# Gathering a mixture-of-experts input in other PSUM banks, with slot tiles ahead of rounding remainders and weight rows in 4 KB pieces

## The chip, the cores and the metric

The kernel runs on one core of one Trainium2 chip. A core has a matrix engine (TensorE, PE in the profile; PEld is its weight load), a vector engine (VectorE, DVE), a scalar engine (ScalarE, ACT), GpSimd (POOL) and SyncE (SP), which here issues nearly all DMAs. They run side by side, each in its own program order, and wait for each other through semaphores. Matmul results land in PSUM, 8 banks of 2 KB in each of 128 partitions. The metric is the device time of one execution in microseconds (us).

## What is computed

Two layers on 256 tokens of width 1024 in fp32: a gated linear attention, then a differential attention, each followed by a layer norm, a mixture of experts and another layer norm. Only the mixture of experts is touched:

```
def hier_moe(x, w_group, b_group, w_router, b_router, w_gate, w_up, w_down):
    ...
    y = jnp.zeros_like(t)
    for e in range(MOE_EXPERTS):            # 16 experts, 1024 -> 512 -> 1024
        hdn = jax.nn.silu(t @ w_gate[e]) * (t @ w_up[e])
        y = y + combine[:, e:e + 1] * (hdn @ w_down[e])
    return y.reshape(B, S, D)
```

Each token goes to the two best of the four experts in its best group; `combine` is zero elsewhere.

## The kernel before

Both layers call `moe`. It runs all 16 experts on at most 64 tokens each; fuller experts get another round in a loop at the end, which this input does not enter, and layer 1 runs one extra block of 64, so 17. An expert's tokens are picked by a matmul with a one-hot matrix (a **slot tile**, `OH`), four experts at a time: that is `gather_group(g)`, for g = 0 before the first expert and for g = 1, 2, 3 ahead of experts 4, 8 and 12. The gather is exact: `split_x` makes of a 128-wide slice of the normalized input `xa` (both token blocks) a rounded high part (`act.activation` on ScalarE, line 534) and the remainder, the **low part** (`eng.tensor_sub` on VectorE, line 535), in a tile `xs` of which there are four. For each of the 8 slices, four matmuls (high part and low part, each for two token blocks) are summed in PSUM (line 553). Two slices share a bank. ScalarE and VectorE then scale, shift and store them as `xg` (lines 560 and 562); the one on ScalarE follows the one on VectorE, since both read the same bank.

PSUM tiles come from three rings: `pA` (4 banks, held by the sums `y` during `moe`), `pB` (2) and `pC` (2). Gather, transposes (`tr_part`, `s_prep`) and half of the down product use `pC`; the gate and up product (`gu_part`, line 610) and the other half of the down product (line 638) use `pB`. A ring hands out its banks in turn, and a writer waits until the last reader of that bank is through.

An expert needs 6 MB of weights: 8 transfers of 512 KB for gate and up (line 282) and 2 of 1 MB for down (line 286). SP issues them in a fixed order into a ring of 16 slots of 1 MB (3 more for the start of each layer), as slots come free, with at most eight transfers under way. The gate and up rows of slot j are `j * 256` to `j * 256 + 255`, partition p holding rows p and p + 128, each 2 KB long. A scheduler puts the instructions of each engine in order from the program text and the `issue_after` hints (`with after(...)`).

Of the kernel before, what the change touches and what calls it, by code (L numbers as in the profile page):

```python
# [10 lines left out]
F32 = mybir.dt.float32  # L11
# [10 lines left out]
KC = D // 128  # L22
# [14 lines left out]
P_G, P_B, P_GN, P_GS, P_WR = 0, 32, 64, 72, 73  # L37
# [6 lines left out]
def body(ctx, tc, x, w_in, wa_out, kv_w, wq, wb_out, wg, wu, wd, gate2, rows, rtab, lng, lnb, cblob, pblob, onehot, out):  # L44
    nc = tc.nc
    pe, act, dve, pool, sp = nc.tensor, nc.scalar, nc.vector, nc.gpsimd, nc.sync

    const = ctx.enter_context(tc.tile_pool(name="const", bufs=1))
# [15 lines left out]
    def pB():  # L64
        return psum.tile([128, 512], F32, tag="B", bufs=2, name=nm("pB"))

    def pC():
        return psum.tile([128, 512], F32, tag="C", bufs=2, name=nm("pC"))
# [7 lines left out]
    xa = const.tile([128, 2, D], F32, name="xa")  # L76
# [5 lines left out]
    iota = cb[:, C_IO:C_IO + 64]  # L82
    pb = const.tile([128, NPB], F32, name="pb")
    rw = const.tile([1, R_LAM], F32, name="rw")
    lnr = const.tile([64, 256], F32R, name="lnr")
    sel_r = const.tile([64, 32], F32R, name="sel_r")
    ones_r = const.tile([128, 128], F32R, name="ones")
# [178 lines left out]
    def load_moe(layer, res):  # L266

        n, spares = 0, []
        for e in range(E):
            gu, dn = [], []  # L270
            res.append((gu, dn))
            for j in range(6):
                if n == RING:
                    spares = yield
                if e == 8 and j == 0:
                    yield
                n += 1
                t = spares.pop(0) if spares else ring_slot()
                if j < 4:
                    t = t.rearrange("p (g k f) -> p g k f", g=2, k=2)  # L280
                    for gi, w in enumerate((wg, wu)):
                        sp.dma_start(t[:, gi], w[layer, e, j * 256:j * 256 + 256].rearrange("(k p) f -> p k f", p=128))
                    gu.append(t)
                else:
                    t = t.rearrange("p (k f) -> p k f", k=2)
                    sp.dma_start(t, wd[layer, e, (j - 4) * 256:(j - 4) * 256 + 256].rearrange("(k p) f -> p k f", p=128))
                    dn.append(t)
        yield
# [32 lines left out]
    rt = sm([32, 8], "rt", bufs=1)  # L321
    sp.dma_start(rt, rtab)
    sp.dma_start(pb, pblob)
    sp.dma_start(rw, rows[0:1, 0:R_LAM])
    for i, w in enumerate((lng, lnb)):
        for j in range(2):
# [142 lines left out]
    def moe(layer, M, lg, rstd, nr, fold, side=None):  # L469
        with tc.tile_pool(name=f"moe{layer}", bufs=1) as mp:  # L470
# [42 lines left out]
            after = lambda i: tc.issue_after(getattr(i, "ins", i)) if i is not None else contextlib.nullcontext()  # L513

            def one_hot(g):
                n = 5 if layer and g == 3 else 4
                OH[g] = mp.tile([128, 2, n, 64], F32R, tag="OH", bufs=2, name=nm("OH"))
                for b in range(2):
                    mm = dve.tensor_tensor(OH[g][:, b, 0:4],
                                      posm[:, b, 4 * g:4 * g + 4].unsqueeze(2).broadcast_to([128, 4, 64]),  # L520
                                      iota.unsqueeze(1).broadcast_to([128, 4, 64]), op=ALU.is_equal)
                    if n == 5:
                        dve.tensor_scalar(OH[g][:, b, 4], iota, extra[1][:, b:b + 1], None, op0=ALU.is_equal)
                return mm
            gcol, bcol = P_G + 16 * layer, P_B + 16 * layer

            lows = []

            def split_x(k, eng, hold=None):

                t = mp.tile([128, 2, 2, 128], F32R, tag="xs", bufs=4, name=nm("xs"))
                x_ = xa[:, :, k * 128:k * 128 + 128]
                with after(hold):
                    act.activation(t[:, 0], x_, AF.Copy)
                lows.append(eng.tensor_sub(t[:, 1], x_, t[:, 0]))
                return t

            def gather_group(g, hold=None, xs=()):

                n = 5 if layer and g == 3 else 4  # L540
                t = mp.tile([128, KC, 256], F32, tag="xg", bufs=1, name=nm("xg"))
                if n == 5:
                    tx = spare_tile(1, [128, KC, 64], F32, "xg4")
                    xg_tiles[4] = tx
                xs = list(xs)
                for k in range(KC):
                    if n == 5 or k % 2 == 0:
                        p = pC()
                    if k >= len(xs):
                        xs.append(split_x(k, dve, hold))  # L550
                    o = p[:, 0:320] if n == 5 else p[:, k % 2 * 256:k % 2 * 256 + 256]
                    for q in range(4):
                        pe.matmul(o, xs[k][:, q // 2, q % 2], OH[g][:, q % 2].rearrange("p e s -> p (e s)"), start=q == 0, stop=q == 3)  # L553
                    for i in range(k, k + 1) if n == 5 else (k - 1, k) if k % 2 else ():
                        src = p[:, 0:256] if n == 5 else p[:, i % 2 * 256:i % 2 * 256 + 256]
                        gc, bc = (pb[:, c + i:c + i + 1] for c in (gcol, bcol))
                        if n == 5:
                            dve.tensor_scalar(tx[:, i], p[:, 256:320], gc, bc, op0=ALU.mult, op1=ALU.add)
                        if n == 5 or i % 2:
                            act.activation(t[:, i], src, AF.Identity, scale=gc, bias=bc)  # L560
                        else:
                            dve.tensor_scalar(t[:, i], src, gc, bc, op0=ALU.mult, op1=ALU.add)
                xg_tiles[g] = t
# [156 lines left out]
            def reload(ei, tile_, eng, et):  # L720

                ev = nc.values_load(ei[0:1, 0:1], engines=[et], min_val=0, max_val=E - 1,
                                    skip_runtime_bounds_check_because="sixteen less a maximum of sixteen down to one")
                ws = []
                for j in range(6):
                    t = tile_(j)
                    if j < 4:
                        t = t.rearrange("p (g k f) -> p g k f", g=2, k=2)
                        for gi, w in enumerate((wg, wu)):
                            eng.dma_start(t[:, gi], w[layer, bass.ds(ev, 1), j * 256:j * 256 + 256].rearrange("e (k p) f -> p (e k) f", p=128))  # L730
                    else:
                        t = t.rearrange("p (k f) -> p k f", k=2)
                        eng.dma_start(t, wd[layer, bass.ds(ev, 1), (j - 4) * 256:(j - 4) * 256 + 256].rearrange("e (k p) f -> p (e k) f", p=128))
                    ws.append(t)
                return ws[:4], ws[4:]

            def overflow(left, base, rev):

                ei, q, cwx = pick(left, base, rev)
                ws, wdn = reload(ei, lambda j: spare_tile(1 + j % 2, [128, 2048], F32, nm("W")), pool, mybir.EngineType.Pool)  # L740
                oh = mp.tile([128, 2, 64], F32, tag="ohw", bufs=2, name=nm("ohx"))
                for b in range(2):
                    dve.tensor_scalar(oh[:, b], iota, q[:, b:b + 1], None, op0=ALU.is_equal)
                st, wsx, _ = s_prep(lambda b: oh[:, b], 64, cwx)
                p = pC()
                pv = p.rearrange("p (k s) -> p k s", k=KC)
                for k in range(KC):
                    for b in range(2):
                        pe.matmul(pv[:, k], xa[:, b, k * 128:k * 128 + 128], oh[:, b], start=b == 0, stop=b == 1)
                xg = mp.tile([128, KC, 64], F32, tag="o", bufs=2, name=nm("xgx"))  # L750
                gv, bv = (pb[:, c:c + KC].unsqueeze(2).broadcast_to([128, KC, 64]) for c in (gcol, bcol))
                dve.tensor_mul(xg, pv, gv)
                dve.tensor_add(xg, xg, bv)
                p = pB()
                gu_part(ws, range(4), lambda k: xg[:, k], p, 2)
                ht, _ = tr_part(act_part(p, 2), 2)
                scatter(st, down_part(wdn, ht, wsx, 2)[0], True)

            xs0 = [split_x(k, dve) for k in range(4)]
            act.activation(sm([128, 2], "warm"), xs0[3][:, 0, 0, 0:2], AF.Exp, scale=0.0)  # L760
            one_hot(0)
            gather_group(0, None, xs0)
            with after(lows[3]):
                cw = combine()
# [1 line left out]
            for e in range(E + layer):  # L766
# [8 lines left out]
                p = pB()  # L775
# [50 lines left out]
            if layer == 0:  # L826
                p = pB()
# [187 lines left out]
    for j in range(2):  # L1015
# [9 lines left out]
        else:  # L1025
            t = mp.tile([128, 2, 4, S], F32R, tag="xhi", name="ogT1")
# [191 lines left out]
```

## Time and profile before

| | |
|---|---|
| median of 3 runs | 770.43 us (769.76 to 772.49) |
| the profiled execution, its own time | 771.24 us |
| its span, first to last instruction | 769.3 us |
| TensorE busy | 727.1 us (95%) |
| VectorE, ScalarE busy | 357.4 us (46%), 296.8 us (39%) |
| read from HBM | 245.77 MB |

Times inside the execution count from the start of the span; layer 0's mixture of experts lies at about 131 to 366 us, layer 1's at about 502 to 758 us. The 1.9 us between the profiled time and its span lie outside the instructions.

### The profile page before, as it was taken

The numbers are of one execution on the slowest core, as the hardware profiler recorded it, in microseconds if no ns is written. First come the engines' busy times: TensorE is split into PE (matmuls) and PEld (weight loads), VectorE is DVE, ScalarE is ACT, GpSimd is POOL, SyncE is SP. The second block draws the span as 40 slices with busy tenths as digits, with TensorE's granted clock in tenths as the row PEclk, the third lists the DMA queues.
The fourth block names the chain that finished last, engine by engine and source line by source line (L and its number), as shares of the span: only waits on it lengthen the run. The fifth ranks groups of instructions, "written<-read, shape, count | busy, mean of one in ns | idle before, by whom it ended". The sixth has DMA issues, their size and how long they took to land. (4 is left out here: it accounts for less than half of the span.)

```text
span 769.3 us, 10560 instructions
## 1 busy us (share of the span) xinstructions
PE 727.1 (95%) x3743; PEld 407.8 (53%) x3743; DVE 357.4 (46%) x959; ACT 296.8 (39%) x651; POOL 8.9 (1%) x21
## 2 busy tenths in 40 slices
PE   7999998999999999999999999999999999999993
PEld 5898776434333434434798877753343343343331
DVE  3655766333263332322758877654235332332225
ACT  4554766323212322222666656552232232232123
POOL 2200000000000000000000000000000000000000
PEclk9999999999999999999999999999999999999997
DMA  7999957599999999999999355619999999999951
GB/s 226 312 384 388 337 191 262 181 397 394 367 387 392 393 396 395 393 393 367 290 364 359 111 174 209 220 62 389 394 381 395 393 363 384 395 395 393 392 200 55
DMA packets 131934, 247.57 MB, mean 322 GB/s; under 512 B 7932, under 2 KB 38117, under 8 KB 131750
## 3 DMA queue, kind: packets, MB, share of 16 engines
q1 hardware_dynamic: 131270, 244.68, 87.6%
q0 software_dynamic: 176, 1.59, 0.5%
q8 instruction: 31, 0.51, 0.3%
q10 hardware_dynamic: 432, 0.59, 0.2%
q14 instruction: 25, 0.20, 0.1%
HBM read 245.77 MB, written 2.63 MB: 323 GB/s over the span
## 5 line engine op out<-in xcount | busy, mean ns | idle before, releaser
L610 PE MATMUL pB<-W,xg 128*64 128x512 f32 x1056 | 263.6, 600 | 0.0
L610 PEld LDWEIGHTS pB<-W,xg 128*64 128x64 f32 x1056 | 77.3, 138 | 137.9 <-issue 132.3
L638 PE MATMUL pB<-W,ht 128*64 128x512 f32 x248 | 112.6, 594 | 0.0
L638 PE MATMUL pC<-W,ht 128*64 128x512 f32 x248 | 111.5, 592 | 0.0
L647 DVE SCALAR_TENSOR_TENSOR o<-pB,wst,o 64x512 fp32r<-64x512 f32 x31 | 23.1, 744 | 145.3 <-ACT o L646 145.3
L119 DVE TENSOR_TENSOR lo<-W,hi 128x512 fp32r<-128x512 f32 x96 | 66.4, 696 | 37.0 <-PE pA L128 23.9
L118 ACT ACTIVATE hi<-W 128x512 fp32r<-128x512 f32 x96 | 59.3, 629 | 48.3 <-PE pA L129 27.8
L646 ACT ACTIVATE o<-pB,wst 64x512 fp32r<-64x512 f32 x31 | 21.2, 682 | 129.6 <-PE pC L638 101.8
L619 DVE TENSOR_TENSOR hd<-sl,pB 128x256 f32<-128x256 f32 x33 | 13.9, 421 | 102.5 <-ACT sl L617 102.5
L617 ACT ACTIVATE sl<-pB 128x256 f32<-128x256 f32 x33 | 12.7, 385 | 126.0 <-PE pB L610 126.0
L638 PEld LDWEIGHTS pB<-W,ht 128*64 128x64 f32 x248 | 33.3, 137 | 52.4 <-issue 49.3
L553 PE MATMUL pC<-OH,xs 128*128 128x256 f32 (+1 forms) x256 | 39.7, 308 | 7.4 <-DVE ht L629 3.8
L670 PE MATMUL pA<-o,st 128*128 128x512 f32 x132 | 40.9, 431 | 4.3 <-DVE o L664 2.1
L553 PEld LDWEIGHTS pC<-OH,xs 128*128 128x128 f32 x256 | 34.8, 203 | 17.8 <-DVE ht L629 5.2
L638 PEld LDWEIGHTS pC<-W,ht 128*64 128x64 f32 x248 | 33.9, 137 | 19.4 <-issue 18.2
L670 PEld LDWEIGHTS pA<-o,st 128*128 128x128 f32 x132 | 22.4, 191 | 33.3 <-issue 23.5
L129 PE MATMUL pA<-x1Thi,lo 128*128 128x256 f32 x128 | 36.1, 288 | 1.4 <-DVE lo L119 1.2
L127 PE MATMUL pA<-x1Thi,hi 128*128 128x256 f32 x128 | 36.7, 288 | 0.0
L128 PE MATMUL pA<-x1Tlo,hi 128*128 128x256 f32 x128 | 36.2, 284 | 0.0
L128 PE MATMUL pA<-lo,xThi 128*128 128x384 f32 (+1 forms) x96 | 34.3, 357 | 0.0
L129 PE MATMUL pA<-hi,xTlo 128*128 128x384 f32 (+1 forms) x96 | 34.3, 357 | 0.0
L127 PE MATMUL pA<-hi,xThi 128*128 128x384 f32 (+1 forms) x96 | 34.2, 362 | 0.0
(338 smaller groups left out, 1086.2 us busy)
## 6 DMA issues: line engine op xcount, KB each, us to landing
W<-in_moe_w_gate_dram SPq DMA_DIRECT2D x132, 512.0 KB, 11.2
W<-in_moe_w_up_dram SPq DMA_DIRECT2D x132, 512.0 KB, 11.0
W<-in_moe_w_down_dram SPq DMA_DIRECT2D x66, 1024.0 KB, 12.0
W<-in_a_w_in_dram SPq DMA_DIRECT2D x16, 256.0 KB, 5.6
W<-in_a_w_in_dram SPq DMA_DIRECT2D x4, 1024.0 KB, 17.8
W<-in_a_w_out_dram SPq DMA_DIRECT2D x4, 1024.0 KB, 14.4
W<-in_kv_w_dram SPq DMA_DIRECT2D x4, 1024.0 KB, 8.8
W<-in_b_w_q_dram SPq DMA_DIRECT2D x16, 256.0 KB, 5.4
```

Of the source, the lines that this page charges most:

```text
L118: act.activation(hi, src, AF.Copy)
L119: dve.tensor_sub(lo, src, hi)
L127: pe.matmul(o, l[0], r[0], start=first, stop=False, skip_group_check=skip)
L128: pe.matmul(o, l[0], r[1], start=False, stop=False, skip_group_check=skip)
L129: pe.matmul(o, l[1], r[0], start=False, stop=last, skip_group_check=skip)
L553: pe.matmul(o, xs[k][:, q // 2, q % 2], OH[g][:, q % 2].rearrange("p e s -> p (e s)"), start=q == 0, stop=q == 3)
L610: mm = pe.matmul(p[c * m:c * m + m, 0:2 * fw].rearrange("p (g f) -> p g f", g=2), xg(k), w[:, :, kk, c * fw:c * fw + fw], start=k == 0, st ...
L619: anchor[1] = dve.tensor_mul(h, sl, p[:, fw:2 * fw])
L638: mm = pe.matmul(p[2 * c // nt][c * m:c * m + m, 0:w], ht[:, q % n, (q // n) * m:(q // n) * m + m], wd_[q // 2][:, q % 2, c * w:c * w + w] ...
L646: act.activation(hi, src, AF.Copy, scale=ws[a:a + m, 0:1])
L647: dve.scalar_tensor_tensor(lo, src, ws[a:a + m, 0:1], hi, op0=ALU.mult, op1=ALU.subtract)
L670: mm = pe.matmul(y[b][c], st[:, b * 128:b * 128 + 128], o[c], start=False, stop=last, skip_group_check=True)
```

## The change

Four edits. The gather's PSUM tiles come from `pB` and `pC` in turn, two from each. At the start of `moe` the second half of the slot tile and the first low part stand ahead of the other three low parts, which wait for it (`later`, `rest`). The gate and up rows of slot j are now rows 8p + 2j and 8p + 2j + 1 for partition p, adjacent in memory, so that one piece is 4 KB; pieces of neighbouring partitions are 16 KB apart. So that the input's columns match these rows, slice k of the gather now takes columns 8q + k: `xa_r` reads every eighth fp32 number of `xa`, and the scale and shift columns are loaded for that order into `ngb`, by four small transfers on POOL's queue.

```diff
+    ngb = const.tile([128, 2, 2, KC], F32, name="ngb")
...
-                        sp.dma_start(t[:, gi], w[layer, e, j * 256:j * 256 + 256].rearrange("(k p) f -> p k f", p=128))
+                        sp.dma_start(t[:, gi], w[layer, e].rearrange("(p r) f -> p r f", r=KC)[:, 2 * j:2 * j + 2])
...
+    for layer in range(2):
+        for c, w in enumerate((lng, lnb)):
+            pool.dma_start(ngb[:, layer, c], w[layer, 0].rearrange("(p r) -> p r", r=KC))
...
-            gcol, bcol = P_G + 16 * layer, P_B + 16 * layer
+
+            xa_r = xa.rearrange("p b (q r) -> p b r q", r=KC)
+            gbr = ngb[:, layer]
...
-            def split_x(k, eng, hold=None):
+            def split_x(k, eng, hold=None, later=False):
...
-                x_ = xa[:, :, k * 128:k * 128 + 128]
+                x_ = xa_r[:, :, k]
                 with after(hold):
                     act.activation(t[:, 0], x_, AF.Copy)
-                lows.append(eng.tensor_sub(t[:, 1], x_, t[:, 0]))
+                low = lambda: lows.append(eng.tensor_sub(t[:, 1], x_, t[:, 0]))
+                if later:
+                    return t, low
+                low()
                 return t
...
                     if n == 5 or k % 2 == 0:
-                        p = pC()
+
+                        i = k if n == 5 else k // 2
+                        p = pC() if i // 2 % 2 else pB()
...
-                        gc, bc = (pb[:, c + i:c + i + 1] for c in (gcol, bcol))
+                        gc, bc = (gbr[:, c, i:i + 1] for c in range(2))
...
-            xs0 = [split_x(k, dve) for k in range(4)]
+            xs0, rest = [split_x(0, dve)], []
+            for k in range(1, 4):
+                t, low = split_x(k, dve, later=True)
+                xs0.append(t)
+                rest.append(low)
             act.activation(sm([128, 2], "warm"), xs0[3][:, 0, 0, 0:2], AF.Exp, scale=0.0)
-            one_hot(0)
+
+            with after(one_hot(0)):
+                for low in rest:
+                    low()
             gather_group(0, None, xs0)
```

The overflow loop and its reload of weights are changed in the same way and are not shown.

How the instructions now stand, at three places. First VectorE at the start of layer 0's `moe`, before: `OH` is the slot tile (one row for each token block), `xs` the low parts, `xg` the evacuation of gathered slices, the small tiles `mx`, `ex`, `comb`, `s` and `sg` the combine weights.

```order
L510 SCALAR_TENSOR_TENSOR posm_1694<-sel_1685,pC_1688 128x32
L519 TENSOR_TENSOR OH_1710<-posm_1694,cb 128x256
L535 TENSOR_TENSOR xs_1696<-xa,xs_1696 128x256
L535 TENSOR_TENSOR xs_1699<-xa,xs_1699 128x256
L535 TENSOR_TENSOR xs_1702<-xa,xs_1702 128x256
L535 TENSOR_TENSOR xs_1705<-xa,xs_1705 128x256
L519 TENSOR_TENSOR OH_1710<-posm_1694,cb 128x256
```

And VectorE there after the change, up to the third evacuation (in the changed file line 523 writes the slot tile, 541 the low parts, 573 evacuates):

```order
L523 TENSOR_TENSOR OH_1712<-posm_1699,cb 128x256
L541 TENSOR_TENSOR xs_1701<-xa,xs_1701 128x256
L523 TENSOR_TENSOR OH_1712<-posm_1699,cb 128x256
L541 TENSOR_TENSOR xs_1704<-xa,xs_1704 128x256
L541 TENSOR_TENSOR xs_1706<-xa,xs_1706 128x256
L541 TENSOR_TENSOR xs_1708<-xa,xs_1708 128x256
L579 TENSOR_REDUCE mx_1775<-lg_1650 128x10
L573 TENSOR_SCALAR xg_1718<-pB_1719,ngb 128x256
L581 TENSOR_TENSOR ex_1777<-lg_1650,mx_1775 128x40
L573 TENSOR_SCALAR xg_1718<-pB_1730,ngb 128x256
L541 TENSOR_TENSOR xs_1742<-xa,xs_1742 128x256
L541 TENSOR_TENSOR xs_1749<-xa,xs_1749 128x256
```

The slot tile's second half moved ahead of three low parts; two evacuations now stand ahead of the low parts of slices 4 to 7.

Second, TensorE at the same place, before (line 553 gathers, line 610 is the first expert's product):

```order
L553 MATMUL pC_1725<-OH_1710,xs_1705 128x256 x4
L610 MATMUL pB_1785<-W_168,xg_1713 64x512
L553 MATMUL pC_1736<-OH_1710,xs_1737 128x256 x4
L553 MATMUL pC_1736<-OH_1710,xs_1744 128x256 x4
L553 MATMUL pC_1753<-OH_1710,xs_1754 128x256 x4
L553 MATMUL pC_1753<-OH_1710,xs_1761 128x256 x4
```

And after (564 gathers, 621 is the product):

```order
L564 MATMUL pB_1730<-OH_1712,xs_1708 128x256 x4
L564 MATMUL pC_1741<-OH_1712,xs_1742 128x256 x2
L621 MATMUL pB_1790<-W_173,xg_1718 64x512
L564 MATMUL pC_1741<-OH_1712,xs_1742 128x256 x2
L564 MATMUL pC_1741<-OH_1712,xs_1749 128x256 x4
L564 MATMUL pC_1758<-OH_1712,xs_1759 128x256 x4
L564 MATMUL pC_1758<-OH_1712,xs_1766 128x256 x4
```

Slices 0 to 3 moved to `pB`, slices 4 to 7 stay in `pC`; the product's first matmul slid two matmuls later.

Third, TensorE at the gather for experts 4 to 7 of layer 0, before (line 626 is the transpose of the last expert's hidden values, in `pC`):

```order
L594 MATMUL pC_1999<-ident_r,ohw_1996 128x128 x2
L626 MATMUL pC_2006<-ident_r,hd_1990 128x128 x2
L553 MATMUL pC_2015<-OH_2011,xs_2016 128x256 x4
L553 MATMUL pC_2015<-OH_2011,xs_2023 128x256 x4
L553 MATMUL pC_2032<-OH_2011,xs_2033 128x256 x4
L553 MATMUL pC_2032<-OH_2011,xs_2040 128x256 x4
L610 MATMUL pB_2083<-W_992,xg_2014 64x512
```

And after (605 and 637 are the transposes):

```order
L605 MATMUL pC_2004<-ident_r,ohw_2001 128x128 x2
L637 MATMUL pC_2011<-ident_r,hd_1995 128x128 x2
L564 MATMUL pB_2020<-OH_2016,xs_2021 128x256 x4
L564 MATMUL pB_2020<-OH_2016,xs_2028 128x256 x4
L564 MATMUL pB_2037<-OH_2016,xs_2038 128x256 x4
L564 MATMUL pB_2037<-OH_2016,xs_2045 128x256 x4
L564 MATMUL pC_2054<-OH_2016,xs_2055 128x256 x4
L564 MATMUL pC_2054<-OH_2016,xs_2062 128x256 x4
```

The first two banks of the gather are no longer the two that the transposes have just written.

## Rows read from the trace of the kernel before

**Rows 1.** The page: busy time by engine, and DMA by 40 slices.

```profile
PE 727.1 (95%) x3743; PEld 407.8 (53%) x3743; DVE 357.4 (46%) x959; ACT 296.8 (39%) x651; POOL 8.9 (1%) x21
...
DMA  7999957599999999999999355619999999999951
GB/s 226 312 384 388 337 191 262 181 397 394 367 387 392 393 396 395 393 393 367 290 364 359 111 174 209 220 62 389 394 381 395 393 363 384 395 395 393 392 200 55
```

**Rows 2.** All waits, summed: waiter <- releaser: us in total, times, longest.

```profile
PE pC L553 <- DVE ht L629: 3.8, 6, 0.6
...
PEld pB L610 <- DMA W<-in_moe_w_gate_dram: 1.6, 7, 0.3
```

**Rows 3.** TensorE's timeline, first gather of layer 0: start, length, what [idle before].

```profile
132.64 0.51 PE L553 MATMUL pC<-OH,xs 128*128 128x256 f32 x2
134.27 3.36 PE L553 MATMUL pC<-OH,xs 128*128 128x256 f32 x14 [1.12 <-DVE OH L519]
...
138.65 2.18 PE L553 MATMUL pC<-OH,xs 128*128 128x256 f32 x16
140.75 7.08 PE L610 MATMUL pB<-W,xg 128*64 128x512 f32 x30
```

**Rows 4.** Windows there: length, busy PE, PEld, DVE, ACT, POOL, PEclk, DMA, GB/s.

```profile
135.00:136.00 1.00, 1.00 (x7) 1.00 (x6) 0.50 (x4) 0.42 (x1) 0.00 (x0) 0.50 0.00 0
138.00:139.00 1.00, 0.98 (x5) 0.35 (x4) 1.00 (x4) 1.00 (x3) 0.00 (x0) 1.00 0.00 0
```

**Rows 5.** VectorE's and ScalarE's timelines there.

```profile
132.11 0.42 DVE L519 TENSOR_TENSOR OH<-posm,cb 128x256 fp32r<-128x256 f32 x1
132.46 1.42 DVE L535 TENSOR_TENSOR xs<-xa,xs 128x256 fp32r<-128x256 f32 x4
133.80 0.41 DVE L519 TENSOR_TENSOR OH<-posm,cb 128x256 fp32r<-128x256 f32 x1
134.13 0.18 DVE L568 TENSOR_REDUCE mx<-lg 128x10 f32<-128x40 f32 x1
...
136.17 0.54 DVE L562 TENSOR_SCALAR xg<-pC,pb 128x256 f32<-128x256 f32 x1
...
130.96 1.32 ACT L534 ACTIVATE xs<-xa 128x256 fp32r<-128x256 f32 x4
```

**Rows 6.** TensorE's timeline, gathers for experts 4, 12 (layer 0) and 12 (layer 1).

```profile
187.55 2.18 PE L553 MATMUL pC<-OH,xs 128*128 128x256 f32 x16 [0.63 <-DVE ht L629]
...
192.82 1.50 PE L610 MATMUL pB<-W,xg 128*64 128x512 f32 x5
...
308.88 2.18 PE L553 MATMUL pC<-OH,xs 128*128 128x256 f32 x16 [0.58 <-ACT xg L560]
...
684.91 1.64 PE L553 MATMUL pC<-OH,xs 128*128 128x320 f32 x8 [0.45 <-ACT xg L560]
686.79 0.85 PE L553 MATMUL pC<-OH,xs 128*128 128x320 f32 x4 [0.25 <-ACT xg L560]
```

**Rows 7.** Two lines of the program, min/median/max ns of one instruction.

```profile
L376 DVE TENSOR_REDUCE rsum<-wrg x2: 423/435/447, 21.6 to 29.9; 128x20 f32<-128x160 f32 x2
...
L497 DVE TENSOR_REDUCE rank<-cmp x2: 319/320/320, 130.5 to 502.0; 128x40 f32<-128x160 f32 x2
```

**Rows 8.** Windows with DMA alone: length, PEclk, DMA share, GB/s.

```profile
276.00:285.00 9.00, 1.00 1.05 386
334.00:339.00 5.00, 1.00 1.03 405
361.00:388.00 27.00, 1.00 1.15 291
```

**Rows 9.** Layer 0's last weights: issue on SP, us to landing (median), first use.

```profile
341.82 1.74 SPq L286 DMA_DIRECT2D W<-in_moe_w_down_dram  x2
...
W<-in_moe_w_down_dram SPq DMA_DIRECT2D x2, 1024.0 KB, 12.0
...
359.79 0.43 PE L658 MATMUL pB<-W,ht 128*64 128x256 f32 x1 [0.63 <-DVE ht L629]
```

**Rows 10.** The page: a queue of small transfers, packets, MB, share of 16 engines.

```profile
q10 hardware_dynamic: 432, 0.59, 0.2%
```

More of the change, by code (lines that the diff above doesn't have):

```diff
@@ L729, in reload @@
                         for gi, w in enumerate((wg, wu)):
-                            eng.dma_start(t[:, gi], w[layer, bass.ds(ev, 1), j * 256:j * 256 + 256].rearrange("e (k p) f -> p (e k) f", p=128))
+                            eng.dma_start(t[:, gi], w[layer, bass.ds(ev, 1)].rearrange("e (p r) f -> p (e r) f", r=KC)[:, 2 * j:2 * j + 2])
                     else:
@@ L748, in overflow @@
                     for b in range(2):
-                        pe.matmul(pv[:, k], xa[:, b, k * 128:k * 128 + 128], oh[:, b], start=b == 0, stop=b == 1)
+                        pe.matmul(pv[:, k], xa_r[:, b, k], oh[:, b], start=b == 0, stop=b == 1)
                 xg = mp.tile([128, KC, 64], F32, tag="o", bufs=2, name=nm("xgx"))
-                gv, bv = (pb[:, c:c + KC].unsqueeze(2).broadcast_to([128, KC, 64]) for c in (gcol, bcol))
+                gv, bv = (gbr[:, c].unsqueeze(2).broadcast_to([128, KC, 64]) for c in range(2))
                 dve.tensor_mul(xg, pv, gv)
```

## The prediction

> **What bounds the kernel now.** The page first [rows 1]: TensorE (PE) is busy 95% of the span, VectorE (DVE) 46%, ScalarE (ACT) 39%. Moving work off PE is not on offer here; what can go is time in which PE stands still, and time in which it runs at half its clock. The page's DMA slices stand near 390 GB/s through both mixtures of experts, so the weights keep the queues full there, and the table of waits says whether PE feels it [rows 2]: PE waited for gate and up weights 1.6 us in seven times, never over 0.3. Faster weights alone are thus worth at most 1.6 us. The same table has six waits, 3.8 us, of gather matmuls (line 553) in `pC` for the copy `ht` that empties `pC` after the transposes: 0.63 us for each gather of experts 4, 8 and 12 in two layers.
>
> Then the start of layer 0's `moe` on PE's timeline [rows 3]: two gather matmuls at 132.64, then 1.12 us idle for the second half of `OH`, then 14 matmuls in 3.36 us. The next sixteen take 2.18 us, 0.136 each; at that rate fourteen are 1.9. The windows say why [rows 4]: after the idle stretch the granted clock is 0.50 (1.2 GHz) at 135 us, 1.00 (2.4 GHz) at 138. About 1.4 us is lost to the clock, beside the idle. DVE's timeline shows who is late [rows 5]: first half of `OH` at 132.11, four lows at 132.46 to 133.88, second half at 133.80.
>
> **The change, part by part.**
>
> **The start.** PE resumed 0.47 us after the second half of `OH` began (134.27 against 133.80). With one low ahead of it instead of four, that half begins at 132.80 and PE resumes at 133.27. If PE is dense from there, 14 gathers of 0.136 (1.90), the 1.02 us that lie between the two halves of the gather (137.63 to 138.65) and the last sixteen (2.18, less the 0.08 by which records overlap, since the product begins at 140.75) end near 138.3 instead of 140.75: 2.4 us a layer is the most that the reordering gives. DVE may not keep up. Its lows now read every eighth number, and no row has such a low. Below, it costs nothing. Above, the nearest row is a reduce of 160 elements: strided 435 ns (line 376), contiguous 319 ns (line 497) [rows 7]; 116 ns over 160 elements is 0.72 ns each, 0.185 us for a low's 256. I take this, the only strided row: a low goes from 0.335 (1.34 us for four starts) to 0.52. DVE's chain from 132.11 is then `OH` 0.335, low 0.52, `OH` 0.335, three lows 1.56, `mx` 0.20, `xg` 0.46, `ex` 0.20, `xg` 0.46, four lows 2.08, 0.35 until PE sees the last one, two matmuls 0.27, and 0.2 for banks (lengths are the distances between starts in [rows 5], which are a little shorter than the records; `ex` as `mx`): 6.97 us, the gather done at 139.1. Gain 140.75 - 139.1 = 1.65 a layer, 3.3 in two. ACT's highs read strided too; they were four in 1.32 us from 130.96, and with the same 0.185 each end at 133.0, where the third and fourth are wanted only at 134: hidden by the first half of `OH` and the first low. PE's idle stretch shrinks from 1.12 to about 0.45, and I take it that the clock stays at 1.00.
>
> The Trainium skill bears on the strided low ("Vector Engine (DVE) Microarchitecture Reference", section "Measured stream behaviour on trn2"): full rate needs runs of two adjacent 4-byte words, and a small step at every element was measured at 2.50 ns a column against 1.054. By that a low would cost 0.37 us more, not 0.185, and the sum below would come to about 1 us; the rows' 0.72 ns is half of it, for a reduce.
>
> **The groups.** At experts 4, 8 and 12 the first two banks come from `pB`, last read by a product's activation, and not from the two that `ht` is still leaving [rows 6]. At most all goes: six times 0.63, and at expert 12 in layer 0 the 0.58 behind ACT's `xg`, in layer 1 0.45 and 0.25: 5.1 us. At least nothing. For expert 4: PE ran dry at 187.55 - 0.63 = 186.92 and began the product at 192.82, 5.9 us; without the wait 5.27. In that time DVE must do the four lows that its ring of four doesn't let it do ahead (4 x 0.52) and four evacuations (4 x 0.46), 3.9 us, and with 0.35 of lag, four matmuls and the last evacuation comes to 5.1 to 5.4: just about PE's own time. I take 0.55 of 0.63 at the four of experts 4 and 8, 0.48 at expert 12 in layer 0, 0.5 in layer 1 (its five-slot gather takes a bank per slice): 3.2 us.
>
> **What it adds.** Four transfers on POOL's queue, each 128 pieces of 32 bytes. A queue of small pieces is in the rows [rows 10]: 432 packets for 0.2% of sixteen engines, 0.2% x 769.3 x 16 / 432 = 57 ns a packet. 512 are 1.8 us if all sixteen engines stand still for it while the first x rows load; nothing, if they fall into a gap. They are issued beside other small loads, and I take 0.4. The longer lows also stretch DVE where it is dense, about the gathers' tails: three or four lows of 0.185 off cover once a layer, 0.2, so 0.4.
>
> **Pieces of 4 KB.** Windows with DMA alone [rows 8]: 386 GB/s where gate and up dominate (2 KB pieces), 405 where it is `down` (4 KB already), 291 where pieces are 512 bytes. So gate and up may gain 5%. PE doesn't wait for them [rows 2]; layer 0's last weights are issued at 341.82, land 12.0 us after their issue, near 355, and are used at 359.79 [rows 9]. That margin of 4.8 us is what hides this edit, and it grows. I cost it at nothing.
>
> **The sum** is 3.3 + 3.2 - 0.4 - 0.4 = 5.7 us. The profiled execution took 771.24, 1.9 of it outside its span; 771.24 - 5.7 = 765.5. The median of the runs shown, 770.43, is 0.8 below the profiled one, so I forecast 764.7.
>
> **The rivals.** A measurement of this kernel tells about 0.5% from no change, 3.85 us: faster is below 766.6, slower above 774.3.
>
> *The strided reads are free.* Then DVE is ahead everywhere and both upper bounds hold: 2 x 2.4 + 5.1 = 9.9, 760.5. For it: a DVE low at 0.335 is far from any rate that its reads need to set, and two reduces on different lines are a thin row [rows 7]. Against it: that row.
>
> *The strided reads double a low*, 0.335 to 0.67. The start's chain is 1.2 us longer than mine, gain 0.5 a layer; the four slices on DVE's path in a group cost 0.6 more, leaving 0.2 of 0.63; 1.0 + 0.8 - 0.8 = 1.0, so 769.4. What speaks for it is that a low reads two inputs and writes one [rows 5], the reduce only reads. The skill's rule named above is the same case by another figure, and no row here shows it.
>
> *The clock falls all the same.* The idle stretch doesn't vanish, and before the first gather PE has little to do in either kernel. Then 1.4 us is lost in each layer as now: 5.7 - 2.8 = 2.9, 767.5. Against it: the fall followed the 1.12 us, and gathers behind the 0.63 us waits still took 2.18 for sixteen [rows 6].
>
> *Gate and up come slower.* Pieces are longer, but neighbouring partitions' pieces are now 16 KB apart instead of following each other, which no row here has. Thirteen experts of 4.19 MB in layer 0 take 141 us at 387 GB/s. The margin of 4.8 us [rows 9] less the 2.9 that layer 0 gains is 1.9; what goes beyond, PE waits. Layer 1 taken alike, 2 x (X - 1.9) must pass 5.7 + 3.85 to make the kernel slower: X = 6.7 us, at 369 GB/s. At the middle of the rows' 386 and 291 (338), X is 20 and the time 801; at 386 nothing happens. For it: DMA is full throughout [rows 1], so any loss shows. Against it: the windows' order, by piece size alone [rows 8].
>
> The Trainium skill lists a case of this kind ("DMA: Bandwidth & Descriptors", section "Latency and other measured facts"): row pitches of 512 KiB and up fell to 207 GB/s and less. 16 KB is far below these, and no run here shows such a pitch.
>
> **Chances.** My forecast 0.52, with a range of its own of 761.5 to 766.5: from lows that cost half of mine (2 us more gain, and no cost for the transfers) to transfers at their full 1.8 us. Free strides 0.13, doubled lows 0.15, the clock 0.12, slower weights 0.08. Faster: 0.52 + 0.13 = 0.65; within 0.5%: 0.15 + 0.12 = 0.27; slower: 0.08. A range from 760.5 (free strides) to 769.8 (doubled lows) leaves out the slower weights and what lies beyond the ends.
>
> **What would show it.** On PE's timeline, less than 0.5 us idle before the first gather's third matmul, PEclk 1.00 behind it, the first gather done 1.6 us sooner after the first `OH`; no wait for `ht` before a gather; lows (541 in the changed file) at 0.5 us instead of 0.355; windows of pure weights at or above 386 GB/s; no wait of PE for `W` beyond today's 1.6 us. The prediction is wrong if lows take 0.67, if the clock window at the start still reads 0.50, if the gathers wait for another reader of `pB` (the activation of the last product) as long as they did for `ht`, or if PE begins to wait for weights.

## The result, and the profile after

The changed kernel takes 765.55 us (median of 13 runs), the kernel before 770.48: a ratio of 0.995 over all runs, 95% interval 0.9933 to 0.9967 (the two medians alone give 0.9936). Forecast was 764.7. The profiled execution took 765.29, its span 763.3 (before 771.24 and 769.3).

The page of the changed kernel, the lines that answer to [rows 1], and its groups of the highs (540, ScalarE) and lows (541, VectorE): busy, mean ns of one, idle before.

```profile
PE 726.3 (95%) x3743; PEld 406.5 (53%) x3743; DVE 369.3 (48%) x959; ACT 310.2 (41%) x651; POOL 11.1 (1%) x25
...
GB/s 217 308 381 400 334 204 273 184 411 410 350 399 409 410 407 409 409 409 342 290 383 288 111 153 233 220 63 393 409 350 410 409 377 392 410 408 409 410 133 56
...
L540 ACT ACTIVATE xs<-xa 128x256 fp32r<-128x256 f32 x64 | 40.1, 682 | 0.2
L541 DVE TENSOR_TENSOR xs<-xa,xs 128x256 fp32r<-128x256 f32 x64 | 38.6, 631 | 2.1 <-ACT xs L540 1.9
```

DMA moves 409 GB/s in the experts instead of 394. VectorE is 12 us busier and ScalarE 13, mainly by the strided reads. All waits, as in [rows 2]:

```profile
PEld pB L621 <- DMA W<-in_moe_w_gate_dram: 2.7, 12, 0.3
...
PE pC L564 <- DVE xs L541: 0.5, 2, 0.3
```

No gather waits for `ht` any more. Gate weights arrive at most 0.3 us late, as before, but twelve times instead of seven, 2.7 us in all against 1.6. PE's timeline at the start of layer 0, to set against [rows 3], then VectorE's and ScalarE's first four highs, against [rows 5]:

```profile
132.81 0.65 PE L564 MATMUL pB<-OH,xs 128*128 128x256 f32 x2
133.64 2.14 PE L564 MATMUL pB<-OH,xs 128*128 128x256 f32 x14 [0.18 <-DVE OH L523]
135.78 0.50 PE L564 MATMUL pC<-OH,xs 128*128 128x256 f32 x2
136.43 1.07 PE L621 MATMUL pB<-W,xg 128*64 128x512 f32 x2
137.43 2.37 PE L564 MATMUL pC<-OH,xs 128*128 128x256 f32 x14
139.74 2.79 PE L621 MATMUL pB<-W,xg 128*64 128x512 f32 x12
```

```profile
132.28 0.43 DVE L523 TENSOR_TENSOR OH<-posm,cb 128x256 fp32r<-128x256 f32 x1
132.62 0.63 DVE L541 TENSOR_TENSOR xs<-xa,xs 128x256 fp32r<-128x256 f32 x1
133.15 0.43 DVE L523 TENSOR_TENSOR OH<-posm,cb 128x256 fp32r<-128x256 f32 x1
133.49 1.74 DVE L541 TENSOR_TENSOR xs<-xa,xs 128x256 fp32r<-128x256 f32 x3
...
138.00 1.25 DVE L541 TENSOR_TENSOR xs<-xa,xs 128x256 fp32r<-128x256 f32 x2 [0.41 <-ACT xs L540]
...
131.25 2.35 ACT L540 ACTIVATE xs<-xa 128x256 fp32r<-128x256 f32 x4
```

The idle stretch fell from 1.12 to 0.18 us and fourteen gathers take 2.14 us instead of 3.36. From the first `OH` to the product it is 7.46 us, before 8.64: 1.18 gained. Lows follow each other 0.55 us apart, before 0.335, and the last two start 0.41 us late, behind ScalarE.

Windows of the changed kernel, against [rows 4] and [rows 8] (length, busy PE, PEld, DVE, ACT, POOL, PEclk, DMA share, GB/s):

```profile
135.00:136.00 1.00, 1.00 (x8) 0.78 (x7) 1.00 (x5) 0.91 (x3) 0.00 (x0) 1.00 0.00 0
...
276.00:285.00 9.00, 9.00 (x44) 3.51 (x42) 4.26 (x11) 3.36 (x8) 0.00 (x0) 1.00 1.03 406
...
652.00:653.00 1.00, 1.00 (x4) 0.38 (x6) 0.00 (x0) 0.59 (x1) 0.00 (x0) 0.50 1.03 414
```

The clock stays at 2.4 GHz behind the start. The kernel before had four stretches at 1.2 GHz ahead of its tail, each some 3.4 us long (from 134, 506, 608 and 656 us, read in windows of 1 us); here one is left, at 651. Layer 0's last weights, against [rows 9] (issue on SP, then us to landing, then first use):

```profile
335.63 1.66 SPq L287 DMA_DIRECT2D W<-in_moe_w_down_dram  x2
...
W<-in_moe_w_down_dram SPq DMA_DIRECT2D x2, 1024.0 KB, 11.5
...
357.47 0.43 PE L669 MATMUL pB<-W,ht 128*64 128x256 f32 x1 [0.63 <-DVE ht L640]
```

They land near 349 for a use at 357.5: a margin of 8 us, before 4.8. Faster transfers went into margin alone.

**A ledger.** VectorE multiplies an expert's `hd` once for each of 33 blocks. The starts of two neighbouring ones, compared between kernels, say what was gained between them. VectorE's timeline, `hd` of experts 3 and 4 in layer 0, kernel before:

```profile
185.81 0.42 DVE L619 TENSOR_TENSOR hd<-sl,pB 128x256 f32<-128x256 f32 x1 [3.28 <-ACT sl L617]
...
203.79 0.42 DVE L619 TENSOR_TENSOR hd<-sl,pB 128x256 f32<-128x256 f32 x1 [4.09 <-ACT sl L617]
```

That is 17.98 us before; in the changed kernel it is 17.45, so the gather between them gained 0.53. All places with a gather (us gained; layer 0's start counted from the first `OH`, layer 1's from expert 15 of layer 0; the four kernels below the first row are experiments):

| | start 0 | 4 | 8 | 12 | start 1 | 4 | 8 | 12 | sum |
|---|---|---|---|---|---|---|---|---|---|
| the change | 1.19 | 0.53 | 0.56 | 0.29 | 1.17 | 0.56 | 0.51 | 1.06 | 5.9 |
| banks | 1.37 | 0.93 | 0.94 | 1.18 | 1.44 | 0.92 | 0.90 | 2.43 | 10.1 |
| order | 0.99 | 0.01 | 0.03 | -0.01 | 1.04 | 0.02 | -0.01 | -0.03 | 2.0 |
| banks_order | 2.28 | 0.93 | 0.92 | 1.18 | 2.19 | 0.94 | 0.90 | 2.44 | 11.8 |
| rows | -0.87 | -0.53 | -0.50 | -0.59 | -2.53 | -0.49 | -0.53 | -0.41 | -6.5 |

Between the gathers the experts take the same time to 0.03 us in all of these, but for the two stretches with layer norm work and the residual (behind experts 5, 6 and 9), where the clock or a wait fell differently by up to 1.6 us.

### The profile page after: what moved, and what is told of

The parts are those of the page before. It is cut to its first block, busy times and chain, and to the rows that moved or that the text cites. A ratio compares the mean times of both kernels' runs of the same rounds, so it can differ in the third digit from the quotient of the medians.

```text
span 763.3 us, 10576 instructions
## 1 busy us (share of the span) xinstructions
PE 726.3 (95%) x3743; PEld 406.5 (53%) x3743; DVE 369.3 (48%) x959; ACT 310.2 (41%) x651; POOL 11.1 (1%) x25
## 5 line engine op out<-in xcount | busy, mean ns | idle before, releaser
L540 ACT ACTIVATE xs<-xa 128x256 fp32r<-128x256 f32 x64 | 40.1, 682 | 0.2
L541 DVE TENSOR_TENSOR xs<-xa,xs 128x256 fp32r<-128x256 f32 x64 | 38.6, 631 | 2.1 <-ACT xs L540 1.9
```

What stands on the lines that cost most here:

```text
L541: low = lambda: lows.append(eng.tensor_sub(t[:, 1], x_, t[:, 0]))
```

## The experiments

**Banks alone.** The kernel before with one edit:

```
-                        p = pC()
+                        i = k if n == 5 else k // 2
+                        p = pC() if i // 2 % 2 else pB()
```

> Before with the gather's banks from pB and pC in turn, and nothing else. By the terms of the prediction: no wait for ht before a gather (3.8 us in the kernel before, 0 here), 3.2 to 4.0 us gained, 766.5 to 767.3 us; the idle stretch of 1.1 us before the first gather and the clock of 0.50 behind it stay in both layers. Rival, that the gain of the whole change comes from the starts alone: 770 us or more here.

Measured 762.04 us, ratio 0.9878 (0.9862 to 0.9894): 8.7 us faster, more than twice what the terms gave, and 3.5 us faster than the whole change. The starts gained too, though their idle stretches stood at 1.16 and 1.11 us: against what was expected, the clock did not fall behind them. PE's timeline at the start of layer 0, against [rows 3], and a window there, against [rows 4]:

```profile
135.01 1.94 PE L554 MATMUL pB<-OH,xs 128*128 128x256 f32 x14 [1.16 <-DVE OH L519]
136.79 1.12 PE L554 MATMUL pC<-OH,xs 128*128 128x256 f32 x8
```

```profile
135.00:136.00 1.00, 0.99 (x8) 0.99 (x9) 0.66 (x5) 0.57 (x2) 0.00 (x0) 1.00 0.00 0
```

Fourteen gathers take 1.94 us at 2.4 GHz, where the kernel before took 3.36 us, most of it at 1.2 GHz: that is the gain at this start, 1.37 us, and layer 1's (1.44) is of the same kind. Ahead of the idle stretch PE does the same work in both kernels but for the bank of two gathers, and no run shows that the banks kept the clock up. So of the 10.1 us in the ledger, the 7.3 at experts 4, 8 and 12 are shown to be the banks', and the 2.8 at the starts are not. PE's timeline at expert 4 of layer 0, against [rows 6]:

```profile
185.88 0.38 PE L627 MATMUL pC<-ident_r,hd 128*128 128x128 f32 x2
186.01 2.16 PE L554 MATMUL pB<-OH,xs 128*128 128x256 f32 x16
188.01 1.39 PE L554 MATMUL pC<-OH,xs 128*128 128x256 f32 x10
189.34 1.07 PE L611 MATMUL pB<-W,xg 128*64 128x512 f32 x2
```

The gather begins 0.13 us behind the start of the transposes, whose record lasts 0.38 us. Before, it began 1.01 us behind theirs (187.55 against 186.54), and the trace called 0.63 of that idle, since idle time counts from the end of a record, and records of matmuls that follow each other overlap. In starts the wait was 0.88 us, and that is the gain (0.93) but for 0.05.

**Order alone.** The second edit alone, the four lines of `rest` and `later` at the start of `moe`.

> Before with the second half of the slot tile and the first low ahead of the other lows, and nothing else. By the terms of the prediction: idle before the first gather 0.2 us or less (1.12 before), granted clock 1.00 behind it in both layers, 2.3 to 3.6 us gained (1.2 to 1.8 a layer), 767 to 768 us; the six waits for ht stay at 0.63. Rival, that the clock falls all the same: clock 0.50 again after the start, about 0.5 us gained a layer, 769.5 us.

Measured 770.26 us, ratio 0.9991 (0.9981 to 1.0001): nothing that can be told from zero. PE's timeline at the start of layer 0:

```profile
133.29 2.56 PE L556 MATMUL pC<-OH,xs 128*128 128x256 f32 x16
135.78 1.07 PE L613 MATMUL pB<-W,xg 128*64 128x512 f32 x2
136.78 1.45 PE L556 MATMUL pC<-OH,xs 128*128 128x256 f32 x10
138.16 1.07 PE L613 MATMUL pB<-W,xg 128*64 128x512 f32 x2
139.17 0.74 PE L556 MATMUL pC<-OH,xs 128*128 128x256 f32 x4
139.84 1.07 PE L613 MATMUL pB<-W,xg 128*64 128x512 f32 x2
140.84 0.50 PE L556 MATMUL pC<-OH,xs 128*128 128x256 f32 x2
141.27 1.94 PE L613 MATMUL pB<-W,xg 128*64 128x512 f32 x8
```

Idle and half clock are gone as expected, and 1.0 us is gained a layer, short of the 1.2 to 1.8. In PE's order the second half of the gather is broken up by the product at three places. At each of these places two matmul records of the product stand alone and take 1.0 us, start to start; two in a run take 0.49 (eight in 1.94). The kernel before has one such place, so two more cost about 1.0 us a layer; this is an estimate from these lines. The sum of 2.0 in the ledger is 0.5 in the median. In the profiled execution, 0.8 us shorter than that of the kernel before, the difference lies in the 132 us ahead of the first `OH`, which took 0.65 us more (in the other profiles from 0.07 less to 0.74 more, clock falls aside), and in the block behind expert 6 of layer 1, which took 0.49 more, with the clock falling at 608 us in both. Whether the other executions are like it is not shown.

**Both.** Banks and order, rows as before.

> Both of them, with the rows as before: no strided reads, no new small transfers, pieces of 2 KB. If strided reads cost what the prediction says (0.185 us a low) and longer pieces bring nothing, this is faster than the whole change by 1.5 to 3 us: 762.5 to 764 us, lows at 0.335 us apart. Rival, that the pieces of 4 KB bring time of their own: 766 us or more, and PE waits for gate and up weights longer than in the changed kernel.

Measured 759.74 us, ratio 0.9855 (0.984 to 0.9871): 5.8 us faster than the whole change, and the fastest of the kernels here beside the one that adds matmuls of zeros to it (759.66). The starts gain 2.28 and 2.19 us, close to the bound of 2.4 in the prediction. That 1.37 and 0.99 add up to nearly the same is chance: the 1.37 of banks alone is the clock, which order alone had back too. Beside the new order the banks give 1.29 and 1.15 us, of which some 1.0 is that the product breaks into the gather at one place instead of three. DMA ran at 384 GB/s in a window of 9 us with weights alone (406 with 4 KB pieces), and the waits for gate weights came to 2.6 us, against 2.7 in the whole change: longer pieces shortened none of them.

**The rows alone.** The remaining two edits: the line of the transfers, `xa_r` and `ngb`.

> Before with the gate and up rows in pieces of 4 KB, the strided reads and the four small transfers, and nothing else. If this part only costs: lows 0.55 us apart and four of them ahead of the slot tile's second half, idle before the first gather 1.12 + 0.2 x 4 = 1.9 us, 1.5 to 3 us slower, 772 to 773.5 us, DMA at 409 GB/s in the experts against 394, and still nobody the better for it. Rival, that faster weights are worth something: 770 us or less.

Measured 777.08 us, ratio 1.0071 (1.0048 to 1.0093): 6.3 us slower, twice the expected, since the gathers of experts 4, 8 and 12 lose 0.5 us each too, and since the clock stayed at 1.2 GHz for twice as long at the start of layer 1 (512 to 519 us). PE's and VectorE's timelines at the start of layer 0 (VectorE's first at 132.78):

```profile
135.38 2.46 PE L559 MATMUL pC<-OH,xs 128*128 128x256 f32 x14 [1.75 <-DVE OH L523]
...
132.78 2.21 DVE L541 TENSOR_TENSOR xs<-xa,xs 128x256 fp32r<-128x256 f32 x4
134.91 0.41 DVE L523 TENSOR_TENSOR OH<-posm,cb 128x256 fp32r<-128x256 f32 x1
136.77 0.64 DVE L541 TENSOR_TENSOR xs<-xa,xs 128x256 fp32r<-128x256 f32 x1 [1.11 <-ACT xs L540]
```

Four long lows ahead of `OH` cost 0.63 us of PE's time, where 0.8 was expected; behind it VectorE is not late by itself, but waits 1.11 us for ScalarE's high. That points to a chain through both engines. Next, whether it is the reads at all and not the transfers, and whose.

**Strided reads without the new transfers, and the new transfers without strided reads.** All in layer 1 alone, so that layer 0 stays as it was. The first three start from banks and order:

```
+                xr_ = xa.rearrange("p b (q r) -> p b r q", r=KC)[:, :, k] if layer else x_
-                    act.activation(t[:, 0], x_, AF.Copy)
+                    act.activation(t[:, 0], xr_, AF.Copy)
-                low = lambda: lows.append(eng.tensor_sub(t[:, 1], x_, t[:, 0]))
+                low = lambda: lows.append(eng.tensor_sub(t[:, 1], xr_, t[:, 0]))
```

The second has the first pair of these lines alone, the third the second pair. The fourth is the changed kernel with `x_ = xa[:, :, k * 128:k * 128 + 128] if layer else xa_r[:, :, k]`.

> The kernel with banks and order (759.74 us) with strided reads of the normalized input in layer 1 alone, highs on ACT and lows on DVE, weights and everything else as they were; the columns then no longer fit the weight rows, so layer 1's experts compute other numbers. If the strided reads are what the rows' part costs, layer 1 loses what the whole change lacks there: 1.1 us at the start, 0.4 at each of experts 4 and 8, 1.4 at expert 12, 3.3 us in all, 763 us, with highs at 0.68 us and lows at 0.63. Rival, that the rows' part costs through its transfers (4 KB pieces, 16 KB apart, small loads): within 0.5 us of 759.74.

> The same with the strided reads in the highs on ACT alone, in layer 1; the values differ in the same way. Theory, that a slot tile's chain is high, then low, each one late by its own extra (0.27 and 0.21 us): 0.57 of the loss of the one with both, 1.5 to 2 us. Rival, that DVE alone is the bound, as the prediction had it: under 0.4 us lost.

> The same with the strided reads in the lows on DVE alone, in layer 1; the values differ in the same way. By the chain: 1.2 to 1.6 us lost. By DVE as the bound: all of the loss of the one with both, 3.3 us.

> The changed kernel with contiguous reads of the normalized input in layer 1 alone: 4 KB pieces and small transfers stay, layer 0 as changed, layer 1's experts compute other numbers. If the strided reads are the cost, layer 1's gains are those of the kernel with banks and order (2.2 us at the start, 0.9 at experts 4 and 8, 2.4 at expert 12), 765.5 - 3.3 = 762.2 us. Rival, that the 4 KB pieces cost or gain: the difference to 0.9 at experts 4 and 8 shows it, or the product waits for weights longer than 0.3 us.

In the second, against what was expected of it, the values stay right: its highs come from other columns, but its lows make up for it, so that only the roundings differ. Medians: 765.18, 763.74, 762.81 and 764.72 us. The ledger of layer 1, where the theory has its places (us gained against the kernel before):

| | start | 4 | 8 | 12 | sum |
|---|---|---|---|---|---|
| banks_order | 2.19 | 0.94 | 0.90 | 2.44 | 6.5 |
| after_contig | 2.24 | 0.94 | 0.92 | 2.43 | 6.5 |
| stride_act | 1.63 | 0.81 | 0.77 | 1.54 | 4.8 |
| stride_dve | 1.48 | 0.64 | 0.60 | 1.86 | 4.6 |
| stride_both | 1.18 | 0.57 | 0.52 | 1.11 | 3.4 |
| the change | 1.17 | 0.56 | 0.51 | 1.06 | 3.3 |

With strided reads and nothing else of the rows' edit the places read as in the changed kernel, within 0.05 us; without them, and with all the rest of it, as in banks and order. So the strided reads are the whole price at the gathers, 3.1 us in layer 1, and 4 KB pieces and `ngb` cost and give nothing there. ScalarE's share alone costs 1.7 us, as the chain has it; VectorE's alone costs 1.9, a little over the 1.2 to 1.6 of the chain and far from the 3.3 of a bound. Their sum, 3.6, is near the 3.1 of both, and VectorE is not the bound alone. The medians agree less well (after_contig 764.72 instead of 762.2, stride_both 765.18 instead of 763): in these two the runs lie up to 2.8 us apart, with mean granted clocks of 0.984 to 0.989, and the profiled execution of after_contig, at 0.989, took 762.55. The profiles show which stretch differs: stride_both has 1.2 GHz at 234, 603 and 651 us, banks_order at 32 and 602.

PE's timeline at expert 12 of layer 1, first in stride_both, then in after_contig:

```profile
679.20 0.75 PE L558 MATMUL pB<-OH,xs 128*128 128x320 f32 x4
680.10 0.94 PE L558 MATMUL pB<-OH,xs 128*128 128x320 f32 x4 [0.15 <-ACT xg L565]
681.13 1.24 PE L558 MATMUL pC<-OH,xs 128*128 128x320 f32 x4
682.29 1.07 PE L615 MATMUL pB<-W,xg 128*64 128x512 f32 x2
```

```profile
677.37 1.34 PE L564 MATMUL pC<-OH,xs 128*128 128x320 f32 x8
678.54 1.34 PE L564 MATMUL pB<-OH,xs 128*128 128x320 f32 x8
679.71 0.96 PE L564 MATMUL pC<-OH,xs 128*128 128x320 f32 x4
680.61 1.07 PE L621 MATMUL pB<-W,xg 128*64 128x512 f32 x2
```

With contiguous reads eight matmuls follow each other in 1.17 us, start to start; with strided ones four take 0.90 to 1.16, paced by the slices.

**The residual's idle stretch and the clock.** Banks and order, with matmuls of zeros added into `y` where PE stands idle behind expert 5:

```
+                            with after(mm):
+                                for _ in range({(0, 0): 0, (0, 1): 0, (1, 0): 2, (1, 1): 4}[b, h]):
+                                    zero(y[b][h], False)
```

> The kernel with banks and order, with six matmuls of zeros added into the sums y behind the residual in each layer (two and four, where PE stands idle 0.23 and 1.06 us for the next residual and the next expert's rows). If the clock's fall at 602 us (and at 234 us in some runs) follows that idle stretch: no window below 1.00 there in either layer, about 0.5 to 1.5 us gained for each fall that is gone, 758.2 to 759.2 us against 759.74. Rival, that the fall has to do with something else (a moment of the run): the clock falls there as before, 759.7 us or up to 0.4 us more for the matmuls.

Measured 759.66 us against 759.74: no change. PE's timeline there in layer 1, and two windows of the same kernel:

```profile
600.74 1.03 PE L181 MATMUL pA<-zero_r 128*128 128x512 f32 x4
601.96 1.52 PE L674 MATMUL pA<-o,st 128*128 128x512 f32 x4 [0.19 <-DVE o L651]
```

```profile
602.00:603.00 1.00, 0.94 (x3) 0.51 (x4) 0.70 (x1) 0.00 (x0) 0.00 (x0) 1.00 1.02 410
...
362.00:363.00 1.00, 1.00 (x3) 0.79 (x3) 1.00 (x2) 1.00 (x2) 0.00 (x0) 0.50 1.21 301
```

The idle of 1.06 us is 0.19, and the clock is full at 602, worth 1.5 us there (the block behind expert 6 gained 1.05 instead of losing 0.49). But the clock fell at 361 and at 648 instead, where banks_order had it full behind the same waits. Whether the filler pays is not settled by this.

**The changed kernel again.**

> The changed kernel once more. Its runs stand at 765.2 us (granted clock 0.992 in the mean) or at 769.2 (0.985). If the difference is stretches of 1.2 GHz at other places, a profile of the second kind shows three more of them of 3.4 us and otherwise the same gains and waits in the experts; a profile of the first kind repeats the one stretch at 651 us.

Measured 765.94 us (764.85 to 769.60); the profiled execution was of the first kind (765.04 us) and repeats the first: one stretch at 651 us, every entry of the ledger within 0.06 us. Of its eight runs four lie at 764.85 to 765.21 us with a mean clock of 0.992, four at 766.68 to 769.60 with 0.985 to 0.990. No profile of the second kind was had, so where the clock falls in it stays open.

## Why the prediction was right, and where only its sum was

The forecast of 764.7 was 0.9 us low; the profiled executions differ by 5.95 us, where the sum has 5.7. The waits that it named went or shrank, and the strided reads had a price; but that the sum came so near is in part luck. Without strided reads the edits give 11.8 us, not the 9.9 of the upper bounds, and the strided reads cost 5.9, where the sum lies 4.2 below its bounds: two errors of about 2 us cancelled.

**The start**, 3.3 us in the sum, measured 1.19 + 1.17 = 2.4. The bound of 2.4 a layer held (2.28 and 2.19 without strided reads), but it was put down to the reordering, which alone gave 0.99 and 1.04; the rest needs the banks, to which the prediction gave nothing here. Idle fell to 0.18 and the clock stayed at 1.00, so the rival on the clock did not come true. That the shorter idle is the reason is not shown: with banks alone the clock stayed full behind 1.16 and 1.11 us. The step that failed is the one on ScalarE's highs, "hidden by the first half of `OH` and the first low": the first four were, but those of slices 4 to 7 were not, and VectorE waited 0.41 us for them. From the first `OH` to the product it is 7.46 us, where the chain had 6.97.

**The groups**, 3.2 us, measured 0.53 + 0.56 + 0.29 + 0.56 + 0.51 + 1.06 = 3.5. But "at most all goes", 5.1 us, is no bound: banks alone gained 7.3 at these six. It was made from the idle column, in which a wait of 0.88 us between starts reads 0.63. At expert 12 of layer 1, where a slice takes a bank of its own, it is further off: the eight matmuls from 684.91 took 1.88 us to the next start [rows 6], against 1.17 unhindered, so 0.71 where the column says 0.25.

**The strided reads.** A low's spacing went from 0.335 to 0.55 us, 0.21 more where 0.185 was taken from [rows 7]: right. What was wrong is where it counts. A slot of the ring goes through high, low, matmuls and back, and both the high (2.35 us for four against 1.32 [rows 5], some 0.25 more each) and the low are on that way at every gather; the prediction's price for the highs was nothing. The two cost some 6 us: 11.8 - 5.9 in the ledger, 5.8 in the medians (759.74 against 765.55). Layer 1's half of it was taken apart, layer 0's was not. The rival on doubled lows had both too high: 0.67 us for a low, and 8.9 for the kernel (9.9 - 1.0).

The rule of the Trainium skill that the prediction cited ("Vector Engine (DVE) Microarchitecture Reference", section "Measured stream behaviour on trn2") has 2.50 ns a column where both sources, or the output, step by 24 words at every element, and 1.73 where one source hops by 4 KiB, against 1.054. A low has one strided source, which steps by 8 words, so neither row is quite its case. By the latter, as an estimate, a low's 256 elements would cost 0.17 us more, by the former 0.37; measured is 0.21: the trace is near the figure for one source, and not near the one that the prediction took.

**The free-strides rival**, 760.5, is what banks_order is (759.74). **4 KB pieces** cost nothing at 16 KB apart and are worth nothing: 406 to 409 GB/s against 384 to 394, all of it margin. The sign that PE waits no more than 1.6 us for weights did not hold (2.7 us), but banks_order, with 2 KB pieces, has 2.6. **The small transfers** (0.4 us) can't be told from the start's own variation: the first `OH` stood at 132.23 to 132.44 us with them, at 132.04 to 132.85 without, clock falls aside. **VectorE's dense stretches** (0.4 us) show 0.2: the block behind expert 5 took 0.11 and 0.09 us longer, as in every layer where VectorE's reads were strided (0.09 to 0.13), and in no other.

## What to carry to other kernels

Lay a change of several edits apart and time each: here one edit held most of the gain (8.7 us), one gave 2.3 more beside it, and one gave 5.8 back, while the sum looked like a small success that matched its forecast. The layout that lengthens the DMA pieces was paid for by the readers of the other operand, on both engines of the chain, and with the DMA in margin it bought nothing. When an edit gains where nothing of it was expected, as banks did at the starts, look at the clock there first. And a wait is to be measured from start to start beside an unhindered repetition, since the idle column starts at the end of a record that the next one would have overlapped.

## What the runs showed of the hardware that had not been expected

The clock does not fall behind every idle stretch of the same length. At the two starts it fell behind 1.12 and 1.10 us in the kernel before and behind 1.75 in rows, and stayed full behind 1.16 and 1.11 in banks. Behind the residual of layer 0, PE stood idle 0.57, 0.23 and 1.06 us in banks and in banks_order alike; windows of the two, banks first:

```profile
236.00:237.00 1.00, 1.00 (x3) 0.51 (x4) 0.57 (x1) 0.00 (x0) 0.00 (x0) 0.60 1.03 406
```

```profile
236.00:237.00 1.00, 0.95 (x4) 0.45 (x4) 0.45 (x1) 0.00 (x0) 0.00 (x0) 1.00 1.03 408
```

Between one and four such stretches, all but one of them 3.4 us long, lie in these profiles ahead of the tail, at places that change from kernel to kernel, and by the ledger each costs some 1.0 to 2.2 us. The spread of the runs (759.5 to 761.0 for banks_order, 764.98 to 770.36 for the change) goes with the granted clock (0.992 at 765, 0.983 at 770.36), so most of it is likely the same thing, and single edits below some 2 us are better read from places in the trace than from times. Why one stretch trips it and another doesn't was not found.
